# A two-layer transformer trunk in split fp32: one matmul of 512 columns per stationary block in place of two of 256

## The chip, the core and the metric

The kernel runs on one core of a Trainium2 chip. A core has a matrix engine (TensorE, PE in the profile) that multiplies a loaded stationary block of 128 by 128 with a stream of columns (the moving operand) and adds the result into an accumulator memory (PSUM, used here as 8 banks of 512 fp32 columns on 128 partitions), a vector engine (DVE), a scalar engine (ACT), a third elementwise engine (POOL), a queue that issues most DMAs (SP), and 16 DMA engines. Each matmul of the program becomes, in the trace, a weight load (PEld) of the stationary block and a streaming pass (PE). The metric is the device time of one execution in microseconds (us), lower is better.

## The reference

The input is one sequence of 512 tokens of width 1024, in fp32. Two layers follow, each made of a normalisation, an attention, a residual, a second normalisation and a gated feed-forward block of width 2816, and a last normalisation closes.

```python
def swiglu(h, w_gate, w_up, w_down):
    return (jax.nn.silu(h @ w_gate) * (h @ w_up)) @ w_down

def reference(x, ...):
    for i in range(DEPTH):          # DEPTH = 2
        h = rmsnorm(x, norm_mix[i])
        if i % 2 == 0:
            x = x + window_gqa_sink(h, w_qkv_a[j], w_out_a[j], sink_a[j])
        else:
            x = x + dilated_mixture_attention(h, w_qkv_b[j], w_out_b[j])
        h = rmsnorm(x, norm_ffn[i])
        x = x + swiglu(h, w_gate[i], w_up[i], w_down[i])
    return rmsnorm(x, norm_final)
```

Layer 0 has 16 query heads over 4 key and value heads of width 64, in a band of 128 keys to each side. Layer 1 has three groups of 16 heads each with their own projections (9216 columns in all), whose results are merged by their softmax denominators.

## The kernel before

**Layout.** Activations lie transposed: 8 blocks of 128 features on the partitions, 512 tokens along the columns. A projection to 128 output features is a chain of products over 8 input blocks (11 in the down projection), each with a 128 by 128 block of the weights as the stationary operand and 512 tokens as the moving one, all added into one PSUM bank.

**Split operands.** The large products use the 4-byte operand type `F32R`, and each operand is held as a high part and a low part (`xh`/`xl`, `oh`/`ol`, `wh`/`wl`, and in the feed-forward block also `ah`/`al`, `bh`/`bl`). `mm3` (L121) forms one product out of three: high by high, high by low, low by high. Each of the three is issued in pieces of 256 columns, so a product with a result of 512 columns is six matmuls on the PE, in three pairs; the two of a pair have the same stationary block and each loads it.

**Who calls it.** `unit` (L204: the projections to queries and keys, and the first gate and up blocks), `out_part` (L486 and L1274: attention output projections), `products` inside `conventional` (L880: gate and up blocks 1 to 5 of each layer) and `against` (L833: the down projection) give `mm3` a result of 512 columns. `values` (L229) gives it 256 columns, as does `final` (L526), which forms the last two output blocks of the program in two token halves. In the remaining feed-forward blocks, gate and up are computed by a scheme with fewer multiplications (`strassen`, L732) whose products (`product`, L725) have 256 columns and do not call `mm3`. `score_pair` (L145) forms the layer 0 attention scores straight with `nc.tensor.matmul`, in the same operand type, over 256 or 384 keys: four matmuls in a row, two results with two key parts each.

**What sets the order.** The PE's instructions stand in the order in which the code issues them; attention steps are woven into the projections by hand (`weave`, `spread`, `lined_up`) so that the PE has projection work while softmax runs on DVE, ACT and POOL. For the other engines a scheduler of the compiler chooses the order from its own estimates, except in the stretches marked with `ORDERED` (L870), where DVE and ACT follow the code as well. The weight blocks come by DMA into `wraw`, ACT makes the high part (L97) and DVE the low one (L98), in up to three buffers.

```python
for k, (a, b) in enumerate(((ah, bh), (ah, bl), (al, bh))):
    for c in range(0, out.shape[-1], 256):
        cols = slice(c, c + 256)
        nc.tensor.matmul(out[:, cols], a, b[:, cols], ...)
```

Of the kernel before, what the change touches and what calls it, by code (L numbers as in the profile page):

```python
# [66 lines left out]
def trunk(ctx, tc, xT, gains, sink, tabs, qsc, wunits, wv, outT, outR):  # L67
# [53 lines left out]
    def mm3(out, ah, al, bh, bl, first, last):  # L121

        for k, (a, b) in enumerate(((ah, bh), (ah, bl), (al, bh))):
            for c in range(0, out.shape[-1], 256):
                cols = slice(c, c + 256)
                nc.tensor.matmul(out[:, cols], a, b[:, cols], start=first and k == 0 and c == 0,  # L126
                                 stop=last and k == 2, skip_group_check=True)

# [75 lines left out]
    def unit(u, hi, lo, tag, done, cuts=(0, NK), ahead=False, between=None):  # L204

        def gen():
            tiles = weight_tiles()
            wh, wl = chunks(tiles, (NK, 128))  # L210
            if ahead:
                load(tiles, wunits[u], slice(0, 128 * NK))
                yield
            ps = bank(tag)
            for j in range(NK):
                if j in cuts and not ahead:
                    load(tiles, wunits[u], slice(128 * j, 128 * cuts[cuts.index(j) + 1]), alone=u == 0 and j == 0)
                if j == 0 and between:
                    between()
                mm3(ps, wh[:, j], wl[:, j], hi[:, j, :], lo[:, j, :], j == 0, j == NK - 1)  # L220
                if j == NK - 1:
                    if norm["wait"] is None:
                        done(ps)
                    else:
                        norm["wait"].append(lambda: done(ps))
                yield
        return NK, gen()

    def values(i, col, hi, lo, out, tags="mm mm mm mm", ahead=False):  # L229


        def gen():
            w = [load_unit(wv[2 * i + k], (4, 256), 96, 1 + (i == 0 and k == 0)) for k in range(2)]
            if ahead:
                yield
            for b in range(4):
                tok = slice(128 * b, 128 * b + 128)
                ps = bank(tags.split()[b], "psv")
                for j in range(NK):
                    wh, wl = w[j // 4]  # L240
                    mm3(ps[:, :256], hi[:, j, tok], lo[:, j, tok], wh[:, j % 4], wl[:, j % 4],
                        j == 0, j == NK - 1)
                    if j == NK - 1:
                        nc.scalar.activation(out[:, b, :], ps[:, :256], AF.Copy, scale=norm["r"][:, col + b:col + b + 1])
                    if j % 2:
                        yield
        return 16, gen()
# [101 lines left out]
    with tc.tile_pool(name="l0", bufs=2) as pool:  # L349
# [136 lines left out]
        def out_part(j, lo, hi, w={}, ahead=False):  # L486
            def gen():
                if lo == 0:
                    w[j] = load_unit(wunits[10 + j], (NK, 128))
                    if ahead:  # L490
                        yield
                    out_ps[j] = bank("mm")
                wh, wl = w[j]
                for c in range(lo, hi):
                    mm3(out_ps[j], wh[:, c], wl[:, c], oh[:, c, :], ol[:, c, :], c == 0, c == NK - 1)
                    if c == NK - 1:
                        residual(j, out_ps[j], 1)
                    yield
            return hi - lo, gen()
# [941 lines left out]
```

## Time and profile before

| what | value |
|---|---|
| time, median of 2 runs | 1394.55 us (1394.54 to 1394.55) |
| span of the profiled execution, first to last instruction | 1391.2 us |
| PEld busy | 1364.8 us, 12414 weight loads |
| DVE busy | 854.0 us (61%) |
| ACT busy | 681.3 us (49%) |
| POOL busy | 224.2 us (16%) |
| read from memory | 149.52 MB, 109 GB/s over the span |

The profile has no time of its own around the span, so the 3.35 us between the span of that one execution and the median of the runs stand for what lies around it. The busy time of a matmul in the profile is its own length with modelled end, and consecutive matmuls overlap: a row of the timeline that says 0.28 us for one matmul and a next row that starts 0.11 us later mean that the PE takes one every 0.11 us. The distance between starts, not the mean of one, is the rate.

### The profile page before, as it was taken

What the parts mean: (1) busy time and instruction counts of PE and PEld (TensorE: products, weight loads), DVE (VectorE), ACT (ScalarE), POOL (GpSimd) and SP (SyncE); (2) the same over time, 40 slices, a digit from 0 to 9 for tenths busy, and PEclk for the clock granted to TensorE, in tenths of its full rate; (3) what the DMA queues carried; (4) which work ended last, traced back from release to release, by engine and by line L of the source; (5) the groups of instructions that cost most, each with busy time, mean ns of one, the idle gap of its engine ahead of it and who ended that gap; (6) DMA issues with size and microseconds to landing.
All of it is one profiled execution on the core that took longest, in us unless ns stands there. A gap on an engine that the chain in (4) does not pass through costs nothing.

```text
span 1391.2 us, 29679 instructions
## 1 busy us (share of the span) xinstructions
PE 1380.1 (99%) x12414; PEld 1364.8 (98%) x12414; DVE 854.0 (61%) x1593; ACT 681.3 (49%) x1250; POOL 224.2 (16%) x318
## 2 busy tenths in 40 slices
PE   9999999999999999999999999999999999999998
PEld 9988999999999999999999999999999999999998
DVE  6776558853788356345655565556466884388633
ACT  6766444632556357335545535436354462265522
POOL 1244220200110111011111111211131010021022
PEclk9999999999999999999999999999999999999999
DMA  6110272743773232322222122221136383387122
GB/s 204 61 62 16 88 186 92 196 130 103 197 196 82 90 119 85 108 79 90 73 81 92 62 93 77 78 92 62 62 115 174 116 209 105 109 217 185 64 94 73
DMA packets 61063, 153.63 MB, mean 110 GB/s; under 512 B 8320, under 2 KB 14336, under 8 KB 60928
## 3 DMA queue, kind: packets, MB, share of 16 engines
q1 hardware_dynamic: 49888, 134.28, 29.0%
q0 software_dynamic: 10752, 16.92, 7.5%
q8 instruction: 97, 1.59, 0.5%
q10 hardware_dynamic: 288, 0.52, 0.1%
q14 instruction: 38, 0.31, 0.1%
HBM read 149.52 MB, written 2.17 MB: 109 GB/s over the span
## 4 chain that ended last, share of the span: by engine, by line
PE 94%; DVE 3%; ACT 2%; issue 1%; DMA 0%; POOL 0%; DVEq 0%; SPq 0%; ACTq 0%
PE mm L126 38%; PE mm L729 13%; PE sc L126 11%; PE psv L126 9%; PE sc L729 9%; PE tp L126 5%; PE ov L446 1%; PE sc L1155 1%; PE ovb L1210 1%; PE sc L1096 1%; PE tp L1118 1%; ACT pr L422 1%; DVE pr L415 1%; PE ov L1137 1%; PE sc L148 1%
## 5 line engine op out<-in xcount | busy, mean ns | idle before, releaser
L98 DVE TENSOR_TENSOR wl<-wraw,wh 128x1024 fp32r<-128x1024 f32 (+5 forms) x196 | 212.6, 1089 | 185.1 <-ACT wh L97 181.4
L97 ACT ACTIVATE wh<-wraw 128x1024 fp32r<-128x1024 f32 (+3 forms) x195 | 181.4, 937 | 244.5 <-PE mm L126 136.0
L126 PE MATMUL mm<-xh,wh 128*128 128x256 f32 x1320 | 267.0, 282 | 0.5 <-ACT xh L259 0.5
L126 PE MATMUL mm<-xl,wh 128*128 128x256 f32 x1320 | 260.3, 277 | 0.0
L126 PE MATMUL mm<-xh,wl 128*128 128x256 f32 x1320 | 260.1, 277 | 0.0
L126 PEld LDWEIGHTS mm<-xh,wh 128*128 128x128 f32 x1320 | 201.3, 189 | 2.4 <-issue 0.8
L126 PEld LDWEIGHTS mm<-xl,wh 128*128 128x128 f32 x1320 | 200.8, 189 | 0.3 <-DVE xl L260 0.3
L126 PEld LDWEIGHTS mm<-xh,wl 128*128 128x128 f32 x1320 | 200.5, 188 | 0.0
L686 POOL DMA_DIRECT2D w<-wunits x64 | 56.1, 916 | 418.3 <-DVE l L709 132.0
L126 PE MATMUL psv<-wh,xh 128*128 128x256 f32 x288 | 80.6, 280 | 0.0
L126 PE MATMUL psv<-wl,xh 128*128 128x256 f32 x288 | 79.8, 277 | 0.2 <-DVE wl L98 0.2
L126 PE MATMUL psv<-wh,xl 128*128 128x256 f32 x288 | 79.7, 277 | 0.0
L273 POOL TENSOR_TENSOR ssum<-ssum,tmp 128x512 f32<-128x512 f32 x26 | 45.0, 1729 | 180.3 <-ACT tmp L270 119.6
L729 PE MATMUL mm<-bh,wh 128*128 128x256 f32 x256 | 70.7, 276 | 0.0
L729 PE MATMUL mm<-bl,wh 128*128 128x256 f32 x256 | 70.7, 276 | 0.0
L729 PE MATMUL mm<-bh,wl 128*128 128x256 f32 x256 | 70.7, 276 | 0.0
L729 PE MATMUL sc<-bh,wh 128*128 128x256 f32 x256 | 70.7, 276 | 0.0
L729 PE MATMUL sc<-bl,wh 128*128 128x256 f32 x256 | 70.7, 276 | 0.0
L729 PE MATMUL sc<-bh,wl 128*128 128x256 f32 x256 | 70.7, 276 | 0.0
L729 PE MATMUL mm<-bh,h 128*128 128x256 f32 x256 | 70.7, 276 | 0.0
L729 PE MATMUL mm<-bl,h 128*128 128x256 f32 x256 | 70.7, 276 | 0.0
L729 PE MATMUL mm<-bh,l 128*128 128x256 f32 x256 | 70.7, 276 | 0.0
(242 smaller groups left out, 3710.4 us busy)
## 6 DMA issues: line engine op xcount, KB each, us to landing
wraw<-wunits SPq DMA_DIRECT2D x159, 512.0 KB, 3.2
w<-wunits SPq DMA_DIRECT2D x96, 256.0 KB, 4.5
w<-wunits POOLq DMA_DIRECT2D x64, 256.0 KB, 5.4
wraw<-wv SPq DMA_DIRECT2D x25, 512.0 KB, 3.3
wraw<-wunits SPq DMA_DIRECT2D x28, 192.0 KB, 2.4
x<-xT SPq DMA_DIRECT2D x8, 256.0 KB, 4.5
wraw<-wunits SPq DMA_DIRECT2D x3, 256.0 KB, 5.1
wraw<-wunits SPq DMA_DIRECT2D x2, 384.0 KB, 3.0
```

The costliest lines, as they stand in the source:

```text
L97: nc.scalar.activation(out_h, src, AF.Copy)
L98: nc.vector.tensor_tensor(out_l, src, out_h.bitcast(F32), op=OP.subtract)
L126: nc.tensor.matmul(out[:, cols], a, b[:, cols], start=first and k == 0 and c == 0, stop=last and k == 2, skip_group_check=True)
L148: nc.tensor.matmul(outs[a], qp[a][:, qc], k[a][:, kc], start=first and k is kp, stop=k is low, skip_group_check=True)
L273: eng.tensor_tensor(norm["sum"], norm["sum"], sq, op=OP.add)
L415: nc.vector.tensor_tensor_reduce(out=pr[:, e, :w], in0=ps[hf], in1=tab0[:, off:off + w], scale=SLOPES[heads[e]], scalar=-3e38, op0=OP.add, ...
L422: nc.scalar.activation(pr[:, e, :w + 1], pr[:, e, :w + 1], AF.Exp, bias=m[:, 1, e:e + 1], accum_out=m[:, 2, e:e + 1])
L446: nc.tensor.matmul(ov[64 * hf:64 * hf + 64, 256 * n:256 * n + 256], v0[:, k0 // 128 + kb, vs], st["pt", kb][:, 256 * hf:256 * hf + 256], s ...
L686: nc.gpsimd.dma_start(sums[:, 512 * k:512 * k + 512], v[:, 0:512], accum_op=OP.add)
L729: nc.tensor.matmul(out, a[:, j], b[:, j], start=first and j == 0 and i == 0, stop=j == 3 and i == 2, skip_group_check=True)
L1096: nc.tensor.matmul(out, qk["qs", p][a][:, 128 * t:128 * t + 128], kp[k], start=t == ts[0] and k == 0, stop=k == 1, skip_group_check=True)
L1118: nc.tensor.transpose(tp[:, (nb * a + kb) * 128:(nb * a + kb) * 128 + 128], st["pr", p, ts][:, a, o + 128 * kb:o + 128 * kb + 128], ident)
```

## The change

In `mm3`, pieces are up to 512 columns instead of 256. Where the result has 256 columns (`values`, `final`), nothing differs. Where it has 512, each pair becomes one matmul.

```diff
-            for c in range(0, out.shape[-1], 256):
-                cols = slice(c, c + 256)
+            for c in range(0, out.shape[-1], 512):
+                cols = slice(c, min(c + 512, out.shape[-1]))
                 nc.tensor.matmul(out[:, cols], a, b[:, cols], start=first and k == 0 and c == 0,
                                  stop=last and k == 2, skip_group_check=True)
```

In the program, `mm3` issues 8064 matmuls of 256 columns before; after, it issues 3342 of 512 columns and 1380 of 256. So 3342 pairs are merged and 3342 weight loads are gone. The other PE work, the waits and the DMAs of SP and POOL keep their number and order.

On the PE, in layer 0, around the second group of four 384-column score matmuls (`sc` is a score bank, `kt`/`kl` and `qt` are keys and queries in parts, `mm` a projection bank), before:

```order
L126 MATMUL mm<-xh,wh 128x256 x2
L126 MATMUL mm<-xl,wh 128x256 x2
L126 MATMUL mm<-xh,wl 128x256 x2
L148 MATMUL sc<-kt_407,qt_431 128x384
L148 MATMUL sc<-kl_409,qt_431 128x384
L148 MATMUL sc<-kt_408,qt_432 128x384
L148 MATMUL sc<-kl_410,qt_432 128x384
L126 MATMUL mm<-xh,wh 128x256 x2
```

The same place on the PE in the changed program:

```order
L126 MATMUL mm<-xh,wh 128x512
L126 MATMUL mm<-xl,wh 128x512
L126 MATMUL mm<-xh,wl 128x512
L148 MATMUL sc<-kt_335,qt_359 128x384
L148 MATMUL sc<-kl_337,qt_359 128x384
L148 MATMUL sc<-kt_336,qt_360 128x384
L148 MATMUL sc<-kl_338,qt_360 128x384
L126 MATMUL mm<-xh,wh 128x512
```

Only the pairs differ: two rows of 256 columns become one of 512, at the same place in the order.

Since the scheduler sees other PE instructions, it orders a few elementwise steps of layer 0, and one weight split at the end of layer 0, differently. The largest such place on DVE (`qt` is a query part, `wl` the low part of a weight block, `mst` softmax statistics, `ol` the low part of the attention output):

```order
-L136 TENSOR_TENSOR qt_1015<-tmp,qt_1015 64x512
-L419 SCALAR_TENSOR_TENSOR mst<-mst,nsink 128x2
-L136 TENSOR_TENSOR qt_1016<-tmp,qt_1016 64x512
-L98 TENSOR_TENSOR wl<-wraw,wh 128x1024
+L98 TENSOR_TENSOR wl<-wraw,wh 128x1024
+L419 SCALAR_TENSOR_TENSOR mst<-mst,nsink 128x2
+L136 TENSOR_TENSOR qt_847<-tmp,qt_847 64x512
+L136 TENSOR_TENSOR qt_848<-tmp,qt_848 64x512
 L424 RECIPROCAL mst<-mst 128x2
 L464 TENSOR_TENSOR ol<-ov,oh 128x2x2x128 x2
```

Here the split of a weight block moves ahead of two query splits and of one small softmax step.

## The prediction

> **What bounds the kernel now.** I read the page first: busy times, the 40 slices, the chain that ended last.
>
> ```profile
> span 1391.2 us, 29679 instructions
> PE 1380.1 (99%) x12414; PEld 1364.8 (98%) x12414; DVE 854.0 (61%) x1593; ACT 681.3 (49%) x1250; POOL 224.2 (16%) x318
> PE   9999999999999999999999999999999999999998
> PEclk9999999999999999999999999999999999999999
> PE 94%; DVE 3%; ACT 2%; issue 1%; DMA 0%; POOL 0%; DVEq 0%; SPq 0%; ACTq 0%
> ```
>
> The matrix engine is busy in every slice, and 94% of the chain that ended last is PE work. Next I asked what PE waits for.
>
> ```profile
> PE warm L334 <- POOL ident masks.py:199: 1.4, 1, 1.4
> PE sc L148 <- DVE mst L415: 1.1, 2, 0.9
> PE ov L446 <- DVE mst L415: 1.1, 1, 1.1
> PE mm L126 <- ACT xh L259: 0.5, 1, 0.5
> PE mm L126 <- DVE ol L464: 0.2, 1, 0.2
> PE psv L126 <- DVE wl L98: 0.2, 1, 0.2
> ```
>
> All waits on other engines together are 1.4 + 1.1 + 1.1 + 0.5 + 0.2 + 0.2 = 4.5 us. So the time is the number of PE instructions times the distance at which PE takes them, and the question is what distance a matmul of 512 columns has, against two of 256. A busy PE cannot answer that, since matmuls overlap; the starts in the timeline can. A long run of pairs in the feed-forward block (columns: start us, length us, engine, line, operation, operands, shape, how many):
>
> ```profile
> 299.74 0.39 PE L126 MATMUL tp<-xl,wh 128*128 128x256 f32 x2
> 299.97 0.39 PE L126 MATMUL tp<-xh,wl 128*128 128x256 f32 x2
> ...
> 305.86 0.39 PE L126 MATMUL sc<-xl,wh 128*128 128x256 f32 x2
> ```
>
> From the first to the last of these there are 28 rows of one pair each, so 27 distances in 6.12 us: 0.2267 us for a pair, 0.1133 for one matmul of 256 columns with its own weight load. The 3342 pairs that the change merges take 3342 x 0.2267 = 757.5 us, over half of the span.
>
> **Term 1, the streaming pass.** No row of this trace has 512 columns. The nearest are the layer 0 scores of 384 columns, in the same operand type, four in a row between plain products:
>
> ```profile
> 43.42 0.28 PE L126 MATMUL mm<-xh,wh 128*128 128x256 f32 x1
> 43.53 0.39 PE L126 MATMUL mm<-xl,wh 128*128 128x256 f32 x2
> 43.76 0.39 PE L126 MATMUL mm<-xh,wl 128*128 128x256 f32 x2
> 43.98 0.33 PE L148 MATMUL sc<-kt,qt 128*128 128x384 f32 x1
> 44.15 0.34 PE L148 MATMUL sc<-kl,qt 128*128 128x384 f32 x1
> 44.33 0.34 PE L148 MATMUL sc<-kt,qt 128*128 128x384 f32 x1
> 44.50 0.34 PE L148 MATMUL sc<-kl,qt 128*128 128x384 f32 x1
> 44.67 0.39 PE L126 MATMUL mm<-xh,wh 128*128 128x256 f32 x2
> ```
>
> The four take 44.67 - 43.98 = 0.69 us, 0.1725 each, with nothing waited for (no bracket on the rows). That is what matters most here. If an instruction had a fixed cost that merging saves, the longer one would be cheaper by the column. It is not: 256 columns are 0.443 ns a column, 384 are 0.1725 / 384 = 0.449 ns. The step from 256 to 384 columns costs 0.0592 us, 0.462 ns a column. So I see no fixed part to save. For 512 columns the rows give three values: 0.2267 if the length goes with the columns at the rate of the 256 (no change); 0.1725 x 512 / 384 = 0.2300 at the rate of the 384; and 0.1725 + 0.0592 = 0.2317 on a straight line through both. I take 0.2300, the rate of the row nearest in length, and because there the weight load (below) surely is not what sets the distance. Per pair that is +0.0033 us, and 3342 x 0.0033 = +11.1 us (11.0 to 11.2 by rounding).
>
> **Term 2, the weight loads.** 3342 loads go. What they cost on the path now is read from where they stand:
>
> ```profile
> 299.63 0.30 PEld L126 LDWEIGHTS tp<-xl,wh 128*128 128x128 f32 x2
> 299.86 0.30 PEld L126 LDWEIGHTS tp<-xh,wl 128*128 128x128 f32 x2
> ```
>
> The load for the pair that streams from 299.97 begins at 299.86, 0.11 us ahead, while the matmul before it streams (it began at 299.74 + 0.113). So one load lies beside one matmul of 256 columns and takes about as long. If the stream is the limit, the load is hidden and its removal is worth nothing; I take that, since the 384-column rows have the same load and nearly all the time by the column. If the load is the limit, it is the third rival.
>
> There is one place where loads are not covered: the switch to other work after a plain product.
>
> ```profile
> 664.67 0.39 PE L126 MATMUL mm<-xh,wl 128*128 128x256 f32 x2
> 664.99 0.88 PE L1210 MATMUL ovb<-pt,v 128*64 128x128 f32 x12
> 588.65 0.40 PE L126 MATMUL mm<-xh,wl 128*128 128x256 f32 x2
> 588.89 0.60 PE L1118 MATMUL tp<-ident,pr 128*128 128x128 f32 x4
> ```
>
> At 664.67 the pair is followed after 0.32 us instead of 0.227, at 588.65 after 0.24. With one load fewer in the pair, the next work's loads can begin a matmul earlier and may hide these 0.09 and 0.01 us. By the starts there are 11 switches of the first kind (8 to L1210, 2 to L446, 1 to L1133) and 85 of the second: 11 x 0.09 + 85 x 0.006 = 1.5 us, where 0.006 is the mean excess of the 85. Between 0 and that; I take -1.5 us.
>
> **Term 3, the start.** Until about 9.4 us the matmuls are slower:
>
> ```profile
> 6.16 0.63 PE L126 MATMUL mm<-xh,wl 128*128 128x256 f32 x2
> ...
> 7.44 0.63 PE L126 MATMUL mm<-xh,wl 128*128 128x256 f32 x2
> ```
>
> Three rows in 1.28 us are 0.427 a pair. There are some dozen pairs in this stretch; one matmul of 512 in place of a pair is the same columns, 0 us. The page's granted clock stays at 9 tenths or more here, so it doesn't tell why.
>
> **Term 4, the other engines.** A result of 512 columns is complete with the end of the last matmul, before as after, so no reader starts earlier or later by more than term 1 moves it. Of the reordered DVE steps the largest is this place:
>
> ```profile
> 74.60 0.69 DVE L136 TENSOR_TENSOR qt<-tmp,qt 64x512 fp32r<-64x512 f32 x1 [0.36 <-ACT qt L135]
> 76.22 1.23 DVE L98 TENSOR_TENSOR wl<-wraw,wh 128x1024 fp32r<-128x1024 f32 x1
> ```
>
> The weight split moves ahead, so two query splits of 0.69 us end up to 1.2 us later, and the softmax step waits up to 0.5 us more. PE has woven projections for that time. If the cover is gone, such a delay is one more wait like the two of L148 (1.1 us) or the one of L446 (1.1 us); if an order is better by luck, those go. Bounds: -2.2 and +2.2 us; I take 0. No DMA moves, and SP and POOL keep their order.
>
> **The sum.** 11.1 - 1.5 + 0 + 0 = +9.6 us on the span of 1391.2: 1400.8. The median of the runs shown is 3.35 above that span, so 1404 us, 0.7% above before.
>
> **The rivals.**
>
> *No change.* The stream costs 0.443 ns a column at any length, and the 2 to 4 ns more at 384 columns are a changeover that the 256 hide. The first of the four gaps, 43.98 to 44.15, is 0.17 and thus 256 x 0.443 x 1.5; the next are 0.18, 0.17 and 0.17. Then term 1 is 0 and the time 1393 to 1395.
>
> *Much slower.* What grows from 256 to 384 grows faster still to 512. Set against 0.1067 (half of the 0.2133 that a matmul took in the slow start), a 256 has 0.0066 too much and a 384 has 0.1725 - 0.16 = 0.0125, about double. Doubled again it is 0.025, so 0.2133 + 0.025 = 0.238: +0.0117 x 3342 = +39 us, 1432.
>
> *Faster.* The weight load is what sets the 0.1133: it begins when the matmul before has begun and takes 0.11, and the next matmul can't start before. This would decide as soon as the bare stream of 256 is under 0.11. With half the loads gone the distance is that of the bare stream, which the slow start bounds: if the array then ran at half of its later rate, 512 columns are 0.2133 now. That gives -0.0134 x 3342 = -45 us, 1350; the range of this case goes from there up to 1366. For it: the load lies exactly in the distance. Against it: the 384-column rows, whose load of 0.11 is over long before the next start, still need 0.1725 and not 0.16. If the excess of 384, 0.0125, were a fixed changeover, 512 would be 0.2258, -3 us: no gain either. So the faster case needs those rows to be special.
>
> The Trainium skill has a rule that speaks for this rival: "TensorE: Matmul & The Clock Gate", section "Back-to-back issue gap", gives a warm isolated distance of N / 2.4 + 2.5 ns, so an estimate of 215.8 ns for 512 columns, 10.9 less than the pair, 1358 us in all. The trace disagrees with it at both lengths it has: the rule gives 109 for 256 and 162.5 for 384, the rows 113.3 and 172.5; the skill's examples are in bf16, and these operands have 4 bytes.
>
> **Chances and range.** The 384-column rate or the straight line (1398 to 1412): 0.46. No change (1390 to 1397): 0.25. Faster (1345 to 1366): 0.11; a smaller gain down to that (1366 to 1390): 0.05. Much slower (1412 to 1440): 0.13, of which 0.08 lies over 1422. The range that leaves out two tenths goes from 1388 to 1422; the likeliest case alone has 1398 to 1412. A measurement of this kernel can tell about 2% from no change (1366.7 to 1422.4): faster 0.11, same 0.81, slower 0.08.
>
> **What the profile after would show.** Term 1: the timeline of a feed-forward stretch has rows of 512 columns at 0.230 us; 0.2267 is no change, 0.216 or less the faster rival, over 0.235 the much slower one. Term 2: PEld has 9072 loads (12414 - 3342) and far less busy time at an unchanged span; a drop of the span with it would prove me wrong, as it would show that loads had been the limit. The switch to L1210 follows within 0.02 us of the matmul's own distance. Term 4: waits of PE on DVE stay within 2 to 7 us in all. The prediction falls if the 512-column distance lies outside 0.2258 to 0.235, or if PE waits on something in the feed-forward or layer 1 stretches, where it waits for nothing now.

## The result and the profile after

The changed kernel takes 1413.4 us (1413.36 to 1413.44), against 1394.55 before: a ratio of 1.0138, 95% interval 1.0117 to 1.0158. The prediction was 1404, with a range of 1388 to 1422. In every execution of this case that has both, the time is 1.7 to 1.9 us above the span (1413.36 and 1411.6 here). So about half of the 3.35 us between span and median before is not what lies around the span: the profiled execution before was a quicker one than the two runs of the median. So the spans below differ by 20.4 us and the medians by 18.9.

The page of the kernel after: span, busy times, PE and PEld by slices, and the engines of the chain that ended last.

```profile
span 1411.6 us, 22986 instructions
PE 1402.6 (99%) x9072; PEld 1231.4 (87%) x9072; DVE 855.6 (61%) x1593; ACT 681.9 (48%) x1250; POOL 224.5 (16%) x318
PE   9999999999999999999999999999999999999998
PEld 8878788988999889988888888888878898899987
PE 98%; DVE 1%; DMA 0%; ACT 0%; issue 0%; POOL 0%; DVEq 0%; SPq 0%; ACTq 0%
```

The 3342 weight loads are gone and PEld is busy for 87% of the span instead of 98%, yet PE is as busy as before and the span is 20.4 us longer. DVE, ACT and POOL have the same work. What PE waits for, in the waits of the kernel after (us in total, times, longest):

```profile
PE warm L334 <- POOL ident masks.py:199: 1.4, 1, 1.4
PE mm L126 <- ACT xh L259: 0.4, 1, 0.4
PE mm L126 <- DVE ol L464: 0.2, 1, 0.2
PE psv L126 <- DVE wl L98: 0.2, 1, 0.2
PE sc L148 <- DVE mst L415: 0.2, 1, 0.2
PE ssq L277 <- ACT tmp L270: 0.2, 1, 0.2
```

These are 2.6 us, less than the 4.5 of before. So the time did not go into waits, it went into the distance between matmuls. A run of merged matmuls in the same feed-forward stage, in the timeline of the kernel after (start us, length us, engine, line, operation, operands, shape, how many):

```profile
309.65 0.39 PE L126 MATMUL sc<-xh,wl 128*128 128x512 f32 x1
309.88 0.40 PE L126 MATMUL sc<-xh,wh 128*128 128x512 f32 x1
310.12 0.39 PE L126 MATMUL sc<-xl,wh 128*128 128x512 f32 x1
...
317.81 0.40 PE L126 MATMUL mm<-xl,wh 128*128 128x512 f32 x1
```

First to last are 35 distances in 8.16 us: 0.2331 us for one matmul of 512 columns, where the pair took 0.2267. Between single starts the distance alternates between some 231 and 236 ns.

Adding up all distances in the two traces by the kind of the first matmul shows where the 20.4 us come from:

| from this matmul to the next | before, us | after, us | difference |
|---|---|---|---|
| L126, products with 512 columns, and those of `final` | 789.16 | 791.41 + 15.46 | +17.71 |
| L126, value products (`psv`), 256 columns, unchanged | 143.84 | 147.27 | +3.43 |
| L729, unchanged | 304.64 | 305.32 | +0.68 |
| L433 and L148, unchanged | 37.52 | 36.00 | -1.52 |

The steady distance makes up the first row: over all places in a run of plain products, without waits and switches to other work, a pair took 227.4 ns before (some of the 256-column matmuls ran at 115 to 121 ns, so the mean lies above the 226.7 of the stretch shown), and a merged matmul takes 233.4. That is 3342 x 0.0060 = 20 us, less some 2 us of shorter waits and of switches. The second row was not expected. The first value products of layer 1 between projections, at nearly the same place of the order, in the timelines of the kernel before and of the kernel after:

```profile
602.27 0.28 PE L126 MATMUL psv<-wl,xh 128*128 128x256 f32 x1
...
603.18 0.28 PE L126 MATMUL psv<-wh,xh 128*128 128x256 f32 x1
```

```profile
606.56 0.28 PE L126 MATMUL psv<-wh,xl 128*128 128x256 f32 x1
...
608.91 0.28 PE L126 MATMUL psv<-wl,xh 128*128 128x256 f32 x1
```

Eight distances in 0.91 us are 114 ns before; 20 in 2.35 us are 117.5 after. The instructions and the addresses are the same in both programs; what ran ahead of them differs.

### The profile page after: what moved, and what is told of

Same layout as the page of the kernel before. It is cut to its first block, busy times and chain, and to the rows that moved or that the text cites. A ratio compares the mean times of both kernels' runs of the same rounds, so it can differ in the third digit from the quotient of the medians.

```text
span 1411.6 us, 22986 instructions
## 1 busy us (share of the span) xinstructions
PE 1402.6 (99%) x9072; PEld 1231.4 (87%) x9072; DVE 855.6 (61%) x1593; ACT 681.9 (48%) x1250; POOL 224.5 (16%) x318
## 4 chain that ended last, share of the span: by engine, by line
PE 98%; DVE 1%; DMA 0%; ACT 0%; issue 0%; POOL 0%; DVEq 0%; SPq 0%; ACTq 0%
PE mm L126 41%; PE mm L729 12%; PE sc L126 11%; PE psv L126 10%; PE sc L729 9%; PE tp L126 5%; PE sc L148 1%; PE ov L446 1%; PE sc L1155 1%; PE ovb L1210 1%; PE tp L433 1%; PE sc L1096 1%; PE tp L1118 1%; PE ov L1137 1%; PE tp L1197 0%; PE ssq L277 0%
## 5 line engine op out<-in xcount | busy, mean ns | idle before, releaser
L126 PE MATMUL mm<-xh,wh 128*128 128x512 f32 (+1 forms) x672 | 270.1, 402 | 0.4 <-ACT xh L259 0.4
L126 PE MATMUL mm<-xl,wh 128*128 128x512 f32 (+1 forms) x672 | 264.1, 393 | 0.0
L126 PE MATMUL mm<-xh,wl 128*128 128x512 f32 (+1 forms) x672 | 263.6, 392 | 0.0
L126 PEld LDWEIGHTS mm<-xh,wl 128*128 128x128 f32 x672 | 127.0, 189 | 29.1
L126 PEld LDWEIGHTS mm<-xh,wh 128*128 128x128 f32 x672 | 127.1, 189 | 26.8 <-issue 0.8
L126 PEld LDWEIGHTS mm<-xl,wh 128*128 128x128 f32 x672 | 127.3, 189 | 25.1 <-DVE xl L260 0.5
L126 PE MATMUL psv<-wh,xh 128*128 128x256 f32 x288 | 81.9, 284 | 0.0
L126 PE MATMUL psv<-wl,xh 128*128 128x256 f32 x288 | 81.1, 282 | 0.2 <-DVE wl L98 0.2
L126 PE MATMUL psv<-wh,xl 128*128 128x256 f32 x288 | 81.0, 281 | 0.0
L729 PE MATMUL mm<-bh,l 128*128 128x256 f32 x256 | 70.9, 277 | 0.0
L729 PE MATMUL mm<-bh,h 128*128 128x256 f32 x256 | 70.9, 277 | 0.0
L729 PE MATMUL mm<-bl,h 128*128 128x256 f32 x256 | 70.9, 277 | 0.0
L729 PE MATMUL sc<-bh,wh 128*128 128x256 f32 x256 | 70.8, 277 | 0.0
L729 PE MATMUL mm<-bl,wh 128*128 128x256 f32 x256 | 70.8, 277 | 0.0
L729 PE MATMUL sc<-bl,wh 128*128 128x256 f32 x256 | 70.8, 277 | 0.0
L729 PE MATMUL sc<-bh,wl 128*128 128x256 f32 x256 | 70.8, 277 | 0.0
L729 PE MATMUL mm<-bh,wh 128*128 128x256 f32 x256 | 70.8, 277 | 0.0
L729 PE MATMUL mm<-bh,wl 128*128 128x256 f32 x256 | 70.8, 277 | 0.0
```

Source lines behind the costliest of these rows:

```text
L729: nc.tensor.matmul(out, a[:, j], b[:, j], start=first and j == 0 and i == 0, stop=j == 3 and i == 2, skip_group_check=True)
```

## The experiments

Distances given below are means over all places in a run's trace where the matmuls before and after have the same shape, waits left out. Address differences are worked out from the places of the tiles in the programs. Of each change only the deciding lines are shown. Except for the two halves and the two kernels with shifted weights, the runs are made to read distances, not whole times.

### Which length costs what

The first block of a chain has all columns, the others have one length per chain.

```diff
-                cols = slice(c, min(c + 512, out.shape[-1]))
+                cols = slice(c, min(c + 512 if first else c + width, out.shape[-1]))
```

> Of each chain of plain products with 512 columns only the first block has all columns; the later blocks have one length per chain (512, 480, 448, 416, 384, 352, 320, 288, 272, 256, 240, 224, 192, 128, 64), so the rest of the columns is left out and the whole time says nothing. Read is the distance from one matmul to the next of the same length. Theory A (the moving stream sets the distance above 256 columns, and each further column costs 0.469 ns, the slope from the 113.3 ns of 256 to the 233.3 ns of 512): 480 gives 218, 448 gives 203, 416 gives 188, 384 gives 173, 352 gives 158, 320 gives 143, 288 gives 128, 272 gives 121; 256 and all below stay at 108 to 114, since there one weight load takes that long. Theory B (a second reading step begins beyond 256 columns and beyond 384, at a price of about 6.7 ns each): steps, 272 at 127, 288 at 133, 384 at 173, 416 at 193, 512 at 233. Theory C (the length goes with the columns and nothing else): 64 to 240 fall below 100 ns in proportion.

| columns | 128 | 192 | 240 | 256 | 272 | 288 | 320 | 352 | 384 | 416 | 448 | 480 | 512 |
|---|---|---|---|---|---|---|---|---|---|---|---|---|---|
| distance, ns | 112 | 112 | 112 | 116 | 124 | 133 | 147 | 160 | 174 | 187 | 202 | 216 | 233 |

Two stretches of this run in which the granted clock was 0.5 (179 to 182 and 479 to 500 us) are left out; 64, 128 and 224 columns took 213 ns there. Theory C falls: from 64 to 240 columns all lengths are at 112. Theory A falls between 256 and 384 (288 columns at 133, not 128), theory B at 416 (187, not 193). Measured are 17 ns for the 32 columns after 256, about 14 ns for each 32 columns from 288 to 480, and 17 for the last 32. The 116 of 256 columns is a mixture: some chains run at 113.5 throughout (616.3 us), others at 117.7 (741.0 us). Seen from 117.7 the step to 288 is 15 ns, nearly that of the others; seen from 113.5 it is 20. So it is the quicker of these two paces that favours 256 columns, and the straight line from 113.3 has the right end by its construction only.

### Weight block at other places

```diff
-            wh, wl = chunks(tiles, (NK, 128))
+            width, at = PLANS[turns[0] % len(PLANS)] if u >= 18 else (512, 0)
+            wh, wl = chunks(tiles, (NK, 128), at)
```

> From the first feed-forward block on, the chains of the query, key, gate and up units take turns between matmuls of 512 and of 256 columns, and between places of the weight block in its tile: 0, 4, 8, 12, 16, 20, 24 or 28 columns further. In both programs, the address of the moving operand minus that of the weight block loaded beside it is 64 modulo 128 bytes nearly everywhere; this moves it through all steps of 16 bytes. Theory A (the stream alone sets 512): 512 columns stay at 231 to 236 ns at every place, and 256 at 113 to 119. Theory D (the weight load collides with the stream in memory, and the places are right for 256 only): 512 columns differ by more than 4 ns between places, and at some place a 512 is at or below 227; 256 rises from 113 to 118 or more at the places where the difference is 0 modulo 128 (16 columns).

At 512 columns the places give 230.3 to 233.8 ns, so the load's place hardly counts. At 256 the usual place (difference 64) has 114.8 and all seven others 117.3 to 120.0, not only the one with difference 0, which alone was expected to be slow. Theory A is right for 512, theory D for 256 alone.

### A shorter weight load

```diff
+            a, o = (a, out) if first else (a[:, :feats], out[:feats])
```

> From the first feed-forward block on, the query, key, gate and up units take turns between 512, 384 and 256 columns, and after the first block of a chain between 128, 64 and 32 features, so the weight load has 128, 64 or 32 columns; the other features are left out. Theory A: 512 stays at 233 ns and 384 at 173 with any load. Theory D (the load disturbs the stream): 512 falls toward 220 with the shorter load, by about 7 ns or more at 32. On what sets 256: if it is the load, 256 falls below 113 with a load of 64 and 32 columns, to about 110; if it is the stream, it stays at 113.

With loads of 128, 64 and 32 columns, 512 takes 233.4, 232.7 and 231.5 ns: a load a quarter as long saves 2 ns, so the load is not what makes the long stream slow. 256 takes 116.0, 116.4 and 113.7 and never less than 113, so at this length a shorter load gains nothing below the quicker pace. The pieces of 384 were followed by pieces of 128, so their distance can't be read here.

### Operands of two bytes

```diff
+            if short and not first:
+                a, b = bw, bx
```

> From the first feed-forward block on, half of the query, key, gate and up chains, after their first block, multiply a fixed stationary block and a fixed moving block of 2-byte numbers, so their products are left out; lengths 512, 384 and 256 take turns, and the other half stays 4-byte. Theory A2 (reading 4 bytes a column at full rate is what falls behind): the 2-byte stream needs 0.417 ns a column and 2 to 4 ns, so 512 takes 216, 384 takes 163 and 256 takes 107 to 110 (or what its load takes), beside 233, 173 and 113 to 118 for 4 bytes. If the array or the writing of results is what falls behind, 2-byte matmuls take 233 and 173 too.

The timeline of that run has a stretch of 21 two-byte matmuls in one row:

```profile
179.44 4.71 PE L133 MATMUL mm<-bx,bw 128*128 128x512 bf16 x21
```

The last of them has a length of some 0.38, so 20 distances are 4.33 us: 0.2165. Over the run it is 215.9 ns for 512 and 109.2 for 256, while 4-byte matmuls of 512 have 233.0 (384 has no clean stretch). So neither the streaming of 512 columns as such nor the writing of 512 results is the limit; the 4-byte operand is. (The 2-byte block is a fixed one, read again by each matmul. That this alone makes it quick is unlikely by the run after the next, where 4-byte matmuls that read 128 columns four times stay at 233.3.) A side effect told more: the two new tiles moved the weight tiles by 64 bytes, and 4-byte matmuls of 256 columns whose difference became 0 rose to 119.5 ns, while 512 columns stayed at 232.9.

### Other starts of the stream

```diff
+                from_ = S * j + (at if j < NK - 1 else 0)
+                mm3(ps, wh[:, j], wl[:, j], *[t[:, from_:from_ + S] for t in flat], j == 0, j == NK - 1, width)
```

> From the first feed-forward block on, the query, key, gate and up units take turns between 512 and 256 columns and between starts of the moving operand and of the weight block, both moved by 0, 4, 8, 16, 32, 48, 64, 80, 96 or 112 columns, so that their difference stays at 64 modulo 128 bytes; the last block of a chain alone keeps its moving columns, so these products are not the reference's. Theory S (what matters is the start address of the moving stream itself): 512 falls below 229 ns at some start, or rises above 237, and 256 leaves 113 to 114 at the starts that are no multiple of 128 columns. Theory L (what matters is only where the stream stands against the weight load beside it): 256 stays at 113 to 117 and 512 at 231 to 235 at every start.

512 columns are at 233.0 to 233.4 at all starts but one (16 bytes later, both moved: 228.9), 256 at 113.8 to 117.8. Theory L holds to within 1 ns but for that one start, which the finer run below follows up.

### The same columns again and again

```diff
+                    r = b[:, None, c:c + part].to_broadcast([128, n, part])
```

> From the first feed-forward block on, the query, key, gate and up units take turns between 512 and 256 columns; after the first block of a chain the moving operand is read plainly, or as 128, 32 or 8 columns read again and again to the same length, so the columns of the result repeat and are not the reference's. Theory R (the distance of long 4-byte streams comes from walking through memory, from one stretch of addresses to the next): 512 falls from 233 toward 216 as the part gets shorter, and 256 toward 109. Theory W (each 4-byte column costs the array or its input path this much, wherever it comes from): 512 stays at 233 and 256 at 113 to 117, or both rise because the access has more steps.

The timeline of a chain of that run that reads 8 columns, 32 bytes, 64 times in each matmul:

```profile
595.06 0.38 PE L134 MATMUL mm<-xh,wh 128*128 128x512 f32 x1
595.27 0.38 PE L134 MATMUL mm<-xl,wh 128*128 128x512 f32 x1
...
599.59 0.60 PE L1128 MATMUL tp<-ident,pr 128*128 128x128 f32 x4
```

21 distances in 4.53 us are 0.2157: 4-byte columns at the speed of 2-byte ones. 256 columns fall to 111.7. With 32 columns again and again it is 236.7 and 119.9, with 128 it is 233.3 and 116.0. So a 4-byte column need not cost more than a 2-byte one, and theory W falls: the results are written in plain order throughout, so the addresses that are read make the difference. Theory R holds in its end only. It expected a steady fall as the part gets shorter, but 32 columns, which are no new addresses either, are slower than plain reading. What it is about the addresses is not shown.

### Half of the merges each

Merged are only `products` and `against` (first), or only `unit` and the two `out_part` (second). The rest goes back to pieces of 256; for the first run this is shown at `unit`, and the two `out_part` have the same.

```diff
-                mm3(ps, wh[:, j], wl[:, j], hi[:, j, :], lo[:, j, :], j == 0, j == NK - 1)
+                mm3(ps, wh[:, j], wl[:, j], hi[:, j, :], lo[:, j, :], j == 0, j == NK - 1, 256)
```

> Only the feed-forward products of the first gate and up blocks 1 to 5 and of the down projections are merged (1470 of the 3342 pairs); the attention projections keep two matmuls of 256. If the cost is by the pair at 233.3 - 226.7 = 6.7 ns, the time rises by 9.8 us, to 1404.3; and since nothing is merged beside the value products of layer 1, they stay at 113 to 115 ns. If the whole loss were an effect of attention stages (waits, value products), it would stay at 1395.

1405.07 us, a ratio of 1.0084 (1.0069 to 1.0099) to 1393.13 beside it: +11.9. The 1470 merged matmuls take 343.1 us in the trace against 1470 x 0.2267 = 333.2 for pairs: +9.9, as expected by the pair. Value products are at 115.0, all their distances taken together, where the kernel before has 115.3.

> Only the attention projections and the first gate and up block of each layer are merged (1872 of the 3342 pairs). By the pair 1872 x 6.7 ns = 12.5 us, plus 3.3 us for value products of layer 1 that go from 114 to 118 ns between merged projections, minus about 4.5 us of small waits and switches that the changed program no longer has: 1405 to 1407. The rises of the two halves add up to that of the whole, 18.9 us. If pairs cost nothing here, 1395 or less.

1402.93 us, 1.0072 (1.0055 to 1.0088): +9.8, 2 us under the time that was expected, and 1 to 3 under the rise (10.5 to 12.5 above 1394.55). Value products are at 117.6 (118.0 in the whole change), so merging the projections of the attention is what slows them here. The two halves add to 21.7 us, 2.9 more than the whole, which is within the intervals of the three ratios.

### Finer starts, and other orders

The first run is the one on starts with `m` for the stream and `at` for the load apart; the second reads and writes columns in another order.

```diff
+                    o, r = (t.rearrange(*way[:1], **way[1]) for t in (o, r))
```

> As the run on starts, but finer: the moving operand starts 0, 1, 2, 3, 4, 6, 12 or 20 columns of 4 bytes later with the weight block in its place, or 2 or 4 later with the weight block moved as much; 512 and 256 columns take turns. Theory S2 (what counts is how the stream's start lies within 32 bytes, which the start at 16 bytes, 229 ns, hinted at): starts that are 16 bytes off a multiple of 32 (4, 12, 20 columns) give 512 in 225 to 230 with the weight block moved or not; the others 231 to 236. Theory L2 (the pair of places of stream and load counts): only the start of 4 columns with the load moved as much is at 229, and 4, 12 and 20 with the load in place are at 231 to 234. For 256, any start but 0, 2 with 2, and 4 with 4 is at 117 to 120 by both.

512 columns: with 4 columns (16 bytes) for both 229.2; with the load in place, 4, 12 and 20 columns give 234.6, 234.7 and 231.2, and 1 column gives 238.9. So theory S2 falls and L2 holds for 512 to within 1 ns: a pair of places counts, and its best is 229. For 256 it does not hold: 2 columns with 2 (8 bytes for both) were expected among the quick ones and have 121, though the difference of the addresses is still 64; 4 with 4 have 114, and with the load in place it is 117 to 123. So the quick pace, as a mean, came only with a difference of 64 bytes in all that was tried, but that difference is not enough for it.

> Same products, but in the query, key, gate and up units from the first feed-forward block on the columns of a matmul are read (and written) in another order: two halves taking turns every 4, 8 or 16 columns, or four quarters every 8 columns, beside the plain order, for 512 and 256 columns in turn. Theory R (the walk through memory sets the distance): the order matters, and some order moves 512 by more than 4 ns up or down; where an order reaches 222 or less, a merged matmul would beat a pair. Theory W (the number of 4-byte columns alone): 231 to 236 at every order.

Two halves in turn every 4, 8, 16 columns: 251.9, 243.3, 240.1. Four quarters every 8: 228.4, the lowest and steadiest. The timeline of one such chain:

```profile
717.77 0.39 PE L133 MATMUL mm<-xl,wh 128*128 128x512 f32 x1
718.00 0.39 PE L133 MATMUL mm<-xh,wl 128*128 128x512 f32 x1
...
720.29 0.60 PE L1127 MATMUL tp<-ident,pr 128*128 128x128 f32 x4
```

Eleven distances in 2.52 us are 0.229. The order moves the same 512 columns by 23 ns, as theory R expected; but 228.4 is still above the pair's 226.7. The results are written in the changed order too, so this run and the next cannot tell the reading from the writing.

> Same products and turns as the run on orders, with more of them: 4, 8 or 16 places taking turns every 8 columns; 4 or 8 every 16; 4 or 8 every 32; 8 every 4; 4 every 2; beside the plain order. Theory R2 (short stays at one place and many places help): 8 and 16 places every 8 columns bring 512 from the 228 of 4 places to 224 or less, and 256 to 113 or less; stays of 16 and 32 columns are at 233 to 240. Theory R3 (what helped is the distance of 512 bytes between the 4 places): 8 and 16 places every 8 columns are at 233 or more, and 4 places every 16 or 32 columns are at 228 to 231. If any order brings 512 to 222 or less, a whole kernel with it would beat the kernel before.

4 places every 8 columns repeat with 228.5; 8 and 16 places every 8 have 246 and 234, 4 places every 16 and 32 have 236.7 and 233.4, 8 places every 16 and 32 have 237 and 238, 8 every 4 has 277 and 4 every 2 has 446. Both theories fall, and no order reaches 226. What makes one order slower than another remains open.

### The benefit of the pair taken away

The weight blocks of all plain products with 512 columns lie 16 columns (64 bytes) further in their tiles, in the kernel before and in the changed one. In both without the shift, the address of the moving operand minus that of the weights loaded beside it is 64 modulo 128 bytes at nearly every 4-byte matmul; with it, it is 0 at some 6780 of the kernel before.

```diff
-            wh, wl = chunks(tiles, (NK, 128))
+            wh, wl = chunks(tiles, (NK, 128), 16)
```

> The kernel before, with the weight blocks of all plain products 64 bytes further in their tiles, so that the difference of the addresses of stream and weight load is 0 instead of 64 modulo 128 bytes at some 6780 matmuls. Theory P (two matmuls of 256 owe their 113.3 ns to that difference, and lose it elsewhere): 118.5 to 119.5 each, 6684 x 5.2 to 6.2 ns = 35 to 41 us more, 1429 to 1436. If the place does not matter, 1394.

1425.82 us, 1.0229 (1.0213 to 1.0244). Its timeline has rows of one pair each (first and last of 21):

```profile
306.11 0.40 PE L126 MATMUL tp<-xh,wh 128*128 128x256 f32 x2
...
310.85 0.40 PE L126 MATMUL sc<-xh,wl 128*128 128x256 f32 x2
```

20 distances in 4.74 us: 0.237 a pair; over the run 118.7 ns for one. Theory P holds in kind, with a time 3 us under its range. Part of that is that it set out from 113.3 ns for every 256-column matmul, where the mean over all steady places before is 113.7.

> The changed kernel with the same shift of 64 bytes. Theory P: a matmul of 512 columns does not care (232 to 234 ns), so 1409 to 1416, which is faster than the shifted pairs by 15 to 25 us: the change wins where the addresses are not arranged. If the long stream is slow for another reason that adds to the place, it rises by as much as the pairs do, to 1440 or more.

1417.90 us, 1.0169 (1.0152 to 1.0186) to the kernel before. The timeline of its merged matmuls (first and last of 23):

```profile
305.74 0.39 PE L126 MATMUL sc<-xl,wh 128*128 128x512 f32 x1
...
310.85 0.39 PE L126 MATMUL mm<-ah,wl 128*128 128x512 f32 x1
```

22 distances in 5.11 us: 0.2323. So the long stream has nothing to lose by the shift, the pair loses 10 ns, and the same merge that costs 18.9 us with the weights in the usual place saves 7.9 us with them shifted (the slowest of the four runs of the one, 1418.26, lies well under the quickest of the other, 1425.23). The 15 to 25 us that were expected did not come, and the time lies above 1416: in the shifted merged kernel the unchanged products of L729 take 314.4 us, 117.0 ns each, where the shifted pairs have 304.8 and 113.4. Its value products, on the other hand, take 144.3 us, about as in the kernel before (143.8), though merged projections stand beside them here too.

## Why the prediction was off

**What bounds the kernel** was right: PE's distances set the time, and the whole change is found in them.

**Term 1** is the step that failed, in its size. It took 0.2300 us for 512 columns, "the rate of the row nearest in length", where 0.2333 was measured: 22 us (20 by the mean of all steady places) instead of 11.1 by this step alone. The reading of the 384 columns was too low, and so was the way from there to 512:

- The four distances behind the 0.1725 are 170, 173, 174 and 173 ns in the trace. The first, right behind a pair, is the odd one; the three behind it, from 44.15 to 44.67 in the rows of the prediction, are 0.1733 each. In proportion that gives 0.2311, and on the straight line through 0.1133 it gives 0.2333.
- The chosen value was in proportion to the length, though the rows showed that the rate itself rises with it (0.443 ns a column at 256, 0.449 at 384, and 0.456 was measured at 512).
- "11.0 to 11.2 by rounding" counted the last step only. 0.69 us read from rows with two decimals may be 0.68 to 0.70, which is 0.2267 to 0.2333 for 512 columns, 0 to 22 us.

That the straight line meets the measured value is in part luck. The run on lengths shows no straight line but 14 ns for each 32 columns from 288 to 480 and more at both ends; with 14 for the last 32 as well, 512 would have stood at 230, the value of the prediction. Why the last ones cost more is open. The prediction's own bounds for this distance, 0.2258 to 0.235, held, but they were wide: they stand for -3 to +28 us.

The reason behind the term was also incomplete: I took the 256 as the plain rate and the 384 as much the same. In fact 256 columns have two paces, and the 113.3 ns come only with the weight block 64 bytes off the stream, modulo 128; at every other difference tried the mean is 117 to 123, so two of them cost 234 to 246, no less than a merged one.

**Term 2** was right that the loads are hidden: 3342 fewer, and a load of a quarter of the length changes 512 columns by 2 ns. It was wrong on the longer switches. The rows of the kernel after at such a place:

```profile
671.53 0.39 PE L126 MATMUL mm<-xh,wl 128*128 128x512 f32 x1
671.85 0.33 PE L1210 MATMUL ovb<-pt,v 128*64 128x128 f32 x2
```

The distance is 0.32, as it was for the pair, and 0.087 more than a merged matmul takes elsewhere, not within 0.02 of it: these 11 switches keep their time. At the shorter switches (to L433, L1118 and L1197, 77 of them) a pair took 232.6 ns before and a merged matmul takes 232.0 after, so their small excess is gone, but that is half a microsecond in all. One reading was also off: a single load has 0.19 us in the trace (a row of two has 0.30, with starts 0.113 apart), not 0.11; the 0.11 is the distance between two loads.

**Term 3** (0 at the start) holds: PE reaches the same column of the first products at 13.59 us before and at 13.57 us after. **Term 4** was within its bounds: the waits on other engines fell from 4.5 to 2.6 us. Those on DVE, expected at 2 to 7 us, fell to 0.6.

**Not in the sum** was that matmuls which the change does not touch could change their distance: +3.4 us at the value products. The two halves show that merging the attention projections brings it about in this kernel (115.0 ns with pairs beside them, 117.6 with merged matmuls). But merged neighbours alone are not the cause, since the shifted merged kernel has them too and its value products stay at 115.6; and in the shifted pairs, where nothing is merged, those of 610 to 650 us run at 118. How it comes about is open. The 256-column stream seems to keep one of two paces, 113 or 118, over a whole stretch.

**The rivals.** No change (0.2267) and the faster one, load-bound, fell; the latter by the short loads. The rule of the Trainium skill for the isolated distance, "TensorE: Matmul & The Clock Gate", section "Back-to-back issue gap", holds here to 0.1 ns for 2-byte operands of 512 columns (215.8 by the rule, 215.9 measured) and falls short by 17.5 for 4-byte ones. The measured distance lies between my value and that of the much slower rival (0.238), whose doubling of the excess overshot: it is 0.020, not 0.025.

What stays open is why a long 4-byte stream falls behind and what sets the two paces of the 256 columns: neither the length, nor the start, nor the order in which places take turns followed one of the rules that I set up. No run that does all of the work was faster than the kernel before.

## What to carry to other kernels

Merging saved nothing by itself here, since the trace showed no fixed cost for each instruction. Compare the nearest two lengths first, over many places and to the nanosecond; if the longer has the higher rate by the column, do not extrapolate the rate. A short instruction may owe its speed to how its operands lie in memory: shift one operand by some tens of bytes before judging a change of instruction size, since here the difference changes its sign. And where PE is the bound, add up distances by kind for the unchanged matmuls too.

## What was not expected

- A 4-byte stream of 512 columns takes 233.3 ns in plain order, 215.7 when 8 columns (32 bytes) are read again and again, and 228 to 277 when the same columns are read and written in other orders (446 with a stay of 2 columns).
- Shifting weight blocks by 64 bytes costs the kernel before 31.4 us (1394.41 to 1425.82).
- Identical 256-column matmuls at the same addresses run at 113 or at 118 ns: the value products after the change (+3.4 us), and the products of L729 in the shifted merged kernel (+9.1 us over the merged one). What ran ahead of them differs, but the rule is not known.
